# Mixing stage of a decoder layer: TensorE's order taken from the source, the recurrence spread over the projections

## The chip, the cores and the metric

The kernel runs on one core of one Trainium2 chip. The metric is the device time of one execution in microseconds. Three timed executions of the kernel before gave 2511.76, 2511.89 and 2522.68 us; the median is 2511.89 us. The engines are named as the profile names them: PE is TensorE's matmuls (PEld its weight loads), DVE is VectorE, ACT is ScalarE, POOL is GpSimd and SP is SyncE, which issues every DMA of this kernel in one queue.

## The reference, cut to what matters

One decoder layer on 1024 tokens of width 1024, in f32. The change lies in its middle part, the mixing:

```
h = rms(x); proj = h @ w_in
# columns: [q | f | v | out gate | pool input | merge gate A | merge gate B]
f = lb + (1 - lb) * sigmoid(f_r);  k = 1 - f;  q = silu(q_r)
# 8 heads, state 128x128 each, over time:
S_t = diag(f_t) S_{t-1} + k_t outer v_t;   o_t = S_t^T q_t
o   = rms(o) * silu(og);            y_a = o @ w_branch_a
# 4 channel groups, trailing means over 2, 4, 8, 16 positions minus the token:
mixed = (pooled @ pool_w) * pool_scale;  y_b = mixed @ w_branch_b
x  += (sigmoid(ga) * y_a + sigmoid(gb) * y_b) @ w_out
```

A SwiGLU feed-forward stands before it and another behind it, then a gated embedding and a last norm. Those parts are the same in both kernels.

## The kernel before, in words

**Tiling.** Activations are kept with the feature on the 128 partitions and tokens along the row, as tiles of 512 tokens (a "half"). Every f32 operand of a projection is split in a high and a low part (`split`, L117: a cast on ACT, then the difference on DVE), and a product is three matmuls of 128x512 (`mm3`, L148). I call one 128x512 matmul a *product row*.

**A pair of column blocks.** `pair` (L294) computes two blocks of 128 output columns at once with seven block products instead of eight; each is 12 product rows. Products 1 and 2 come first, then the two that the pair before left over (`rest`, 4 and 3, run by `flush`), then 6, 5, 7. Between them ACT copies banks out (L330, L341, L344) and DVE adds (L81). The weights of a pair are loaded (`raw`), added and subtracted on POOL (L90, L93) and split into `wa`, `ws`, `wd`, `wt`. The tile pools are small (`ROOM`, L32): 12 tiles for weights, 28 for activations, 8 and 5 of half width.

**The mixing stage** (L681 to L999) runs 4 pairs for v (`v_pair`), 8 for q and f (`qf_pair`), 4 for the output gate (`og_pair`), 2 for the pooling input (`pool_pair`) and 8 for the merge gates (`gate_pair`). The results of v, of the gates and of pooling go to DRAM and are loaded back where they are used.

**The recurrence** (`hgrn`, L806) is done for each of 8 heads in two halves, 16 times in all. In one half TensorE does small f32 matmuls in groups of four, one group per bank "aux" (three banks): scores on the diagonal (L822), a transpose of v (L829), seven *levels* (L849), a transpose of k (L875), state updates (L879), the output (L897, L899), and a last transpose (L910), which I call the *turn*. In the profile such a group of four shows as 8 matmul records (4 for a transpose). Each level reads q and k as the level before left them: after a group DVE copies scores out (`copy_predicated`, L852) and multiplies q and k in place (`mul(both, both, by)`, L87 `qk<-qk,tot`), and only then can the next level's matmuls go. Before the turn ACT squares four times (L902), DVE and POOL make a reciprocal root (L161, L162), and DVE scales (L904).

**What sets the order.** In both kernels the instructions of every engine stand in one fixed order when the program runs, and each engine waits at the head of its own row. In the kernel before, a scheduler makes that order for all engines at build time, from priorities in source order and its own estimate of when things are ready. The source runs for each head: the next `qf_pair`, every second time `v_pair` and `og_pair`, then the two halves of `hgrn`, then one or two of `others` (L914). Means of the pooling groups are one function, `pool_group` (L751), called when a group's input is complete. At the end come the four `m` tiles (L936), `branch_b` for 8 column blocks with `load_act` between (L984), and the branch A pairs.

## Time and profile before

| | us |
|---|---|
| median of three timed executions | 2511.89 |
| the profiled execution, its own time | 2514.3 |
| its span, first to last instruction | 2512.6 |
| PE busy | 2363.0 (94%) |
| DVE busy | 1554.5 (62%) |
| ACT busy | 974.3 (39%) |
| POOL busy | 446.2 (18%) |
| mean granted TensorE clock | 0.975 of full |

The profiled execution took 2.4 us more than the median, and its span is 1.7 us short of its own time. Its timeline has the mixing stage from 726 us (first product row of its first pair, beside the second half of the norm) to about 1660 us. The first recurrence group starts at 824 us, the last one at 1518 us, and the last product row of branch B starts at 1558 us. "PE busy" is no measure of useful work: the records of neighbouring matmuls overlap, so waits are read from the view of waits (who waited for whom) and from the number of matmuls in a stretch of time. "PEclk" is the clock that was granted to TensorE.

### The profile page before, as it was taken

To read this page: it belongs to the slowest core of one execution; us is meant where nothing else is said; L and a number is where in the kernel's file an instruction comes from. 1 tells how busy PE (TensorE), PEld (TensorE's weight loads), DVE (VectorE), ACT (ScalarE), POOL (GpSimd) and SP (SyncE) were. 2 spreads that over 40 slices of the span, in tenths; PEclk is the share of its full clock that TensorE was granted. 3 is DMA by queue.
4 is the path that set the end of the run, shared out by engine and by line. 5 is a ranking of instruction groups with operands and counts; after the bars stand their busy time and mean duration, and the time that the engine had idled before them with its cause. 6 is when DMAs were issued, how large, how long until landed. Compare 5 with 4: busy or idle time off the path is not lost.

```text
span 2512.6 us, 29499 instructions
## 1 busy us (share of the span) xinstructions
PE 2363.0 (94%) x11003; PEld 1925.0 (77%) x11003; DVE 1554.5 (62%) x2138; ACT 974.3 (39%) x1511; POOL 446.2 (18%) x390
## 2 busy tenths in 40 slices
PE   7899999999998999989999988989899999999987
PEld 5688788877777778768778767867688888877776
DVE  5745555577776665674564675576645544577767
ACT  7433333332274334233333332236433333343375
POOL 2222322100013212122222101201322222000000
PEclk9999999999998999999999989999999999999999
DMA  5244444463432213222312346753235533644234
GB/s 206 93 155 157 157 171 147 166 227 118 126 122 84 87 48 108 69 87 82 101 61 83 117 138 211 229 196 126 101 109 164 176 103 98 239 164 139 93 107 153
DMA packets 133952, 334.11 MB, mean 133 GB/s; under 512 B 15280, under 2 KB 15792, under 8 KB 133808
## 3 DMA queue, kind: packets, MB, share of 16 engines
q1 hardware_dynamic: 133808, 332.23, 39.3%
q8 instruction: 86, 1.41, 0.2%
q14 instruction: 58, 0.48, 0.1%
HBM read 230.98 MB, written 101.19 MB: 132 GB/s over the span
## 4 chain that ended last, share of the span: by engine, by line
PE 73%; DVE 12%; ACT 4%; DMA 4%; issue 3%; POOL 3%; SPq 0%; POOLq 0%; DVEq 0%; ACTq 0%
PE pA L151 12%; PE pA L152 11%; PE pA L150 11%; PE pB L151 5%; PE pB L152 5%; PE pB L150 5%; PE aux L849 4%; PE pC L151 3%; PE pC L152 3%; PE pC L150 3%; PE aux L152 2%; PE aux L151 2%; PE aux L150 2%; DVE qk L87 1%; DVE rB L84 1%
## 5 line engine op out<-in xcount | busy, mean ns | idle before, releaser
L90 POOL TENSOR_TENSOR s<-rb 128x512 f32<-128x512 f32 x74 | 101.8, 1376 | 690.4 <-PE pA L152 355.0
L119 DVE TENSOR_TENSOR wtl<-rb,wth 128x1024 fp32r<-128x1024 f32 x74 | 90.7, 1225 | 154.3 <-ACT wth L118 151.4
L118 ACT CAST wsh<-s 128x1024 fp32r<-128x1024 f32 x74 | 77.8, 1051 | 227.4 <-POOL s L93 216.1
L93 POOL TENSOR_TENSOR rb<-ra,s 128x512 f32<-128x512 f32 x74 | 96.7, 1307 | 381.5 <-DVE wd L119 373.1
L849 PEld LDWEIGHTS aux<-qk 128*128 128x128 f32 (+1 forms) x896 | 107.6, 190 | 46.0 <-issue 28.7
L118 ACT CAST wth<-rb 128x1024 fp32r<-128x1024 f32 x74 | 77.6, 1048 | 157.9 <-POOL rb L93 157.9
L118 ACT CAST w2h<-rB 128x1024 fp32r<-128x1024 f32 x72 | 68.6, 976 | 177.0 <-DVE rB L84 152.8
L849 PE MATMUL aux<-qk 128*128 128x64 f32 (+1 forms) x896 | 115.1, 273 | 18.4 <-DVE qk L87 17.3
L119 DVE TENSOR_TENSOR wsl<-s,wsh 128x1024 fp32r<-128x1024 f32 x74 | 90.5, 1223 | 65.0 <-ACT wsh L118 54.3
L150 PE MATMUL pA<-xT1h,wsh 128*128 128x512 f32 x280 | 112.6, 402 | 17.6 <-ACT xT1h L118 17.6
L118 ACT CAST wah<-ra 128x1024 fp32r<-128x1024 f32 x74 | 77.9, 1053 | 127.5 <-PE pC L151 79.2
L150 PE MATMUL pA<-xT3h,wth 128*128 128x512 f32 x296 | 118.7, 401 | 3.7 <-ACT g L341 2.4
L150 PE MATMUL pB<-xT1h,wsh 128*128 128x512 f32 x296 | 117.5, 397 | 2.8 <-DVE o L81 1.1
L152 PE MATMUL pB<-xT1h,wsl 128*128 128x512 f32 x296 | 118.5, 400 | 0.0
L150 PE MATMUL pC<-x0h,wah 128*128 128x512 f32 x296 | 116.9, 395 | 1.5 <-ACT x0h L118 1.3
L152 PE MATMUL pA<-x0h,wal 128*128 128x512 f32 x296 | 116.6, 394 | 1.8 <-DVE wal L119 1.7
L151 PE MATMUL pB<-xT1l,wsh 128*128 128x512 f32 x296 | 117.5, 397 | 0.3 <-DVE xT1l L119 0.3
L151 PE MATMUL pC<-x0l,wah 128*128 128x512 f32 x296 | 116.7, 394 | 0.9 <-DVE x0l L119 0.9
L151 PE MATMUL pA<-xT3l,wth 128*128 128x512 f32 x296 | 117.4, 397 | 0.0
L150 PE MATMUL pA<-x0h,wah 128*128 128x512 f32 x296 | 117.3, 396 | 0.0
L211 POOL TENSOR_TENSOR rs<-rs,mhalf 128x1 f32<-128x1 f32 x16 | 10.7, 667 | 600.4 <-DVE rs L210 600.4
L152 PE MATMUL pA<-xT3h,wtl 128*128 128x512 f32 x296 | 117.1, 396 | 0.0
(338 smaller groups left out, 6768.8 us busy)
## 6 DMA issues: line engine op xcount, KB each, us to landing
ra<-in_ffn_w_dram SPq DMA_DIRECT2D x50, 512.0 KB, 3.7
rb<-in_ffn_w_dram SPq DMA_DIRECT2D x44, 512.0 KB, 4.0
gsS<-gs SPq DMA_DIRECT2D x88, 256.0 KB, 2.2
rB<-in_ffn_w_dram SPq DMA_DIRECT2D x40, 512.0 KB, 4.3
gr<-gsS SPq DMA_DIRECT2D x40, 512.0 KB, 4.3
gsA<-g SPq DMA_DIRECT2D x66, 256.0 KB, 2.0
gr<-gsA SPq DMA_DIRECT2D x30, 512.0 KB, 4.0
ra<-in_w_in_dram SPq DMA_DIRECT2D x29, 512.0 KB, 3.7
```

Source lines behind the costliest of these rows:

```text
L84: nc.vector.tensor_tensor(o, x, y, ALU.subtract)
L87: nc.vector.tensor_tensor(o, x, y, ALU.mult)
L90: nc.gpsimd.tensor_tensor(o, x, y, ALU.add)
L93: nc.gpsimd.tensor_tensor(o, x, y, ALU.subtract)
L118: nc.scalar.copy(hi, src)
L119: nc.vector.tensor_tensor(lo, src, hi.bitcast(F32), ALU.subtract)
L150: nc.tensor.matmul(ps, ah, bh, start=first, stop=False, **kw)
L151: nc.tensor.matmul(ps, ah, bl, start=False, stop=False, **kw)
L152: nc.tensor.matmul(ps, al, bh, start=False, stop=last, **kw)
L211: nc.gpsimd.tensor_tensor(rs, rs, mhalf[:, :1], ALU.pow)
L849: nc.tensor.matmul(ps[:m, c, :64], kc[c][:, :m], right, start=True, stop=True)
```

## The change

- **TensorE's order in the mixing is the source's.** The heads' part is put in `tc.manual_schedule(engines={nc.tensor.engine})`; on the other engines the scheduler still chooses. `pair`, `hgrn` and `branch_b` become generators: `yield False` stands behind each three product rows of a pair (28 such *parts* in a pair), and `hgrn` yields behind each of its 13 groups of a half. `among` deals 84 parts (88 in heads 0 and 2, 74 in head 7) evenly over a head's 26 groups.
- **The turn is put off.** It becomes a closure that runs behind the third group of the next half (`i == 2`).
- **Order of the pairs.** v goes first of the three pairs at the start (before: the q and f pairs of heads 0 and 1, then v; now v, q and f of head 0, output gate), and with heads 1, 3 and 5 run the v and output-gate pairs of the next two heads and the q-f pair of the next. The pooling pairs go with heads 0 and 2, the last two gate pairs and branch B's first block (`branch_b(0)`) with head 7.
- **Pooling means in steps.** `pool_means` yields after each half of each window step and is advanced once per part of the next pair (`beside_means`); its tiles come from the weights' pool (both halves in one tile). `pool_maps` then does the maps; `pool_w` is loaded and split twice instead of once.
- **Tiles.** The state is kept in `f`'s tile instead of a new one; `og` is loaded behind the group that updates the state (before: at the half's start); branch B's gate tile is loaded from the other half-width pool and its product is written in place, and its banks are "pA" alone (before: three "aux" and two "pA" in turn).
- **Order of DMAs.** `load` can be held behind a given DMA in SP's row (`tc.issue_after`): the `m` tiles behind what was issued last before them, and the loads behind the recurrence behind the last `og` load.

```diff
-    def load(dst, src):
-        nc.sync.dma_start(out=dst, in_=src)
+    behind, latest = [None], [None]
+
+    def load(dst, src, at_once=False):
+        with ExitStack() as turn:
+            if behind[0] is not None and not at_once:
+                turn.enter_context(tc.issue_after(behind[0]))
+            latest[0] = nc.sync.dma_start(out=dst, in_=src).ins
         return dst
...
                 mm3(ps, hi[:, c], lo[:, c], *act[b][k], start and k == 0, k == 3)
+                yield False
...
+    def beside_means(it):
+        for part in it:
+            yield part
+            while means and next(means[0], 0) == 0:
+                means.pop(0)
...
-        og = load(t_("h", "og"), og_dram[h][half])
...
+        og = load(t_("h", "og"), og_dram[h][half], True)
+        og_last[0] = latest[0]
         befores = []
-        for c, (s_, p_) in enumerate(zip(chunks(t_("h", "st")), chunks(ps))):
+        for c, (s_, p_) in enumerate(zip(chunks(f), chunks(ps))):
...
-        ps = bank("aux")
-        for p_, a_ in zip(chunks(ps), qc):
-            nc.tensor.transpose(p_, a_, ident)
-        nc.vector.scalar_tensor_tensor(og, ps, onorm[:, h : h + 1], og, ALU.mult, ALU.mult)
-        store(o_dram[h][half], og)
+        def turn():
+            ps = bank("aux")
+            for p_, a_ in zip(chunks(ps), qc):
+                nc.tensor.transpose(p_, a_, ident)
+            nc.vector.scalar_tensor_tensor(og, ps, onorm[:, h : h + 1], og, ALU.mult, ALU.mult)
+            store(o_dram[h][half], og)
+        turns.append(turn)
...
+    GROUPS = 2 * 13
+    def head(h):
+        for half in range(2):
+            for i, _ in enumerate(hgrn(h, half)):
+                if i == 2 and turns:
+                    turns.pop(0)()
+                yield
+    def among(its, groups, n):
+        parts = (p for it in its for p in it if not p)
+        done = 0
+        for i, _ in enumerate(groups, 1):
+            while done * GROUPS < i * n:
+                next(parts, None)
+                done += 1
+        for _ in parts:
+            pass
...
-            ps = bank(BANKS_B[n_b[0] % len(BANKS_B)], "yb")
+            ps = bank("pA", "yb")
...
+    with tc.manual_schedule(engines={nc.tensor.engine}):
+        for h in range(HEADS):
+            its = more[h]() if h in more else (v_pair(h + 1), qf_pair(h + 1), og_pair(h + 1))
+            among(its, head(h), (74 if h == 7 else 3 * PAIR + 4 * (h in (0, 2))))
+        turns.pop(0)()
+    behind[0] = og_last[0]
```

TensorE, between the two halves of head 0 in the kernel before. `pC` rows are product rows of a pair, `aux` rows are recurrence groups; the turn of the first half (L910) stands 11 product rows behind that half's output matmuls:

```order
L150 MATMUL pC_6549<-x0h_5391,wah_6528 128x512
L151 MATMUL pC_6549<-x0l_5392,wah_6528 128x512
L910 MATMUL aux_6300<-ident,qk_5509 128x128 x4
L822 MATMUL aux_6312<-qk_5510 128x128 x4
L829 MATMUL aux_6318<-ident,v_6308 128x128 x4
L152 MATMUL pC_6549<-x0h_5391,wal_6529 128x512
L150 MATMUL pC_6549<-x0h_5411,wah_6528 128x512
L151 MATMUL pC_6549<-x0l_5412,wah_6528 128x512
L152 MATMUL pC_6549<-x0h_5411,wal_6529 128x512
L150 MATMUL pC_6549<-x0h_5431,wah_6528 128x512
L849 MATMUL aux_6333<-qk_5510 128x64 x4
L151 MATMUL pC_6549<-x0l_5432,wah_6528 128x512
```

The same engine in the changed kernel, second half of head 1, from its first level (now L886) to the second, with the turn (now L957) of the first half (`qk_6233`) behind the level:

```order
L886 MATMUL aux_7057<-qk_6234 128x64 x4
L957 MATMUL aux_7062<-ident,qk_6233 128x128 x4
L157 MATMUL pA_6933<-xT1h_5766,wsh_6920 128x512
L158 MATMUL pA_6933<-xT1l_5767,wsh_6920 128x512
L159 MATMUL pA_6933<-xT1h_5766,wsl_6921 128x512
L157 MATMUL pA_6933<-xT1h_5795,wsh_6920 128x512
L158 MATMUL pA_6933<-xT1l_5796,wsh_6920 128x512
L159 MATMUL pA_6933<-xT1h_5795,wsl_6921 128x512
L157 MATMUL pB_7040<-xT1h_5636,wsh_6920 128x512
L158 MATMUL pB_7040<-xT1l_5637,wsh_6920 128x512
L159 MATMUL pB_7040<-xT1h_5636,wsl_6921 128x512
L886 MATMUL aux_7081<-qk_6234 128x64 x4
```

Two neighbouring levels had mostly 4 to 6 product rows between them and now have 9 or 12 (6 at some places of head 7). Between a half's output matmuls and its turn stood 10 to 14 product rows in 13 of the 16 halves; now 24 or more product rows and three small groups stand there, 18 product rows for the last half. Runs of recurrence groups without a product row between fell away, and the blocks of small matmuls among product rows rose from 173 to 193.

TensorE at the end of the recurrence, head 7's second half, in the kernel before; `yb` is branch B:

```order
L910 MATMUL aux_10727<-ident,qk_9871 128x128 x4
L822 MATMUL aux_10739<-qk_9872 128x128 x4
L829 MATMUL aux_10745<-ident,v_10735 128x128 x4
L849 MATMUL aux_10760<-qk_9872 128x64 x4
L849 MATMUL aux_10767<-qk_9872 128x64 x4
L849 MATMUL aux_10774<-qk_9872 128x64 x4
L849 MATMUL aux_10781<-qk_9872 128x64 x4
L849 MATMUL aux_10788<-qk_9872 128x64 x4
L150 MATMUL pC_11461<-x0h_11306,wah_11440 128x512
L849 MATMUL aux_10795<-qk_9872 128x64 x4
L151 MATMUL pC_11461<-x0l_11307,wah_11440 128x512
L152 MATMUL pC_11461<-x0h_11306,wal_11441 128x512
```

The end of the same half in the changed kernel, with branch B's first block around the output matmuls:

```order
L943 MATMUL aux_11004<-f_9861,qk_9859 128x128
L941 MATMUL aux_11004<-v_10790,score_5506 128x128
L943 MATMUL aux_11004<-f_9861,qk_9859 128x128
L941 MATMUL aux_11004<-v_10790,score_5506 128x128
L943 MATMUL aux_11004<-f_9861,qk_9859 128x128
L157 MATMUL yb_10992<-mh_10691,wb_10987 128x512
L158 MATMUL yb_10992<-ml_10692,wb_10987 128x512
L159 MATMUL yb_10992<-mh_10691,wb_10987 128x512
L157 MATMUL yb_10992<-mh_10705,wb_10987 128x512
L158 MATMUL yb_10992<-ml_10706,wb_10987 128x512
L159 MATMUL yb_10992<-mh_10705,wb_10987 128x512
L157 MATMUL yb_11023<-mh_10684,wb_10987 128x512
```

Head 7's second half had only a handful of product rows among its groups; its levels now lie among the last gate pair's.

DVE in the pooling of head 2's time, changed kernel, from within one window step (`pw`, L81) to the multiplication of a level (`pb` and `pwhl` are the splits for the maps):

```order
L81 TENSOR_TENSOR pw_7758<-pw_7740 128x4
L87 TENSOR_TENSOR pw_7758<-pw_7758,invc 128x8
L799 SCALAR_TENSOR_TENSOR o_7321<-pw_7758,o_7321 128x504
L84 TENSOR_TENSOR o_7321<-pw_7758,o_7321 128x8
L799 SCALAR_TENSOR_TENSOR o_7322<-pw_7758,o_7322 128x512
L81 TENSOR_TENSOR f_7523<-f_7523,pB_7663 128x512
L119 TENSOR_TENSOR pwhl_7776<-pwr_7774,pwhl_7776 128x512
L119 TENSOR_TENSOR pb_7779<-o_7324,pb_7779 128x512
L718 TENSOR_SCALAR f_7523<-f_7523,lb_126,lb 128x512
L119 TENSOR_TENSOR pb_7788<-o_7323,pb_7788 128x512
L890 COPY_PREDICATED score_5506<-mask_81,aux_7753 128x64x4
L87 TENSOR_TENSOR qk_6906<-qk_6906,tot_7685 128x2x64x4
```

In the kernel before, all window steps of a group stand in DVE's row one behind the other, with the turn's scaling among them. In the changed kernel they stand between levels, but at this place 13 other DVE rows still lie between one level's multiplication and the next level's score copy.

More of the change, by code (lines that the diff above doesn't have):

```diff
@@ L288, in hybrid_block, with flushed @@
     waiting = []
+    def flushed():
+        while waiting:
+            yield from waiting.pop(0)()
     def flush():
-        while waiting:
-            waiting.pop(0)()
+        for _ in flushed():
+            pass
     def pair(wa, wb, act, tiles, on11, on22, on21, on12, early=False):
@@ L348, in rest @@
         def rest():
-            product(4, pa, False)
+            yield from product(4, pa, False)
             on21(pa)
-            product(3, pb, False)
+            yield from product(3, pb, False)
             add(c2, c2, pb)
@@ L357, in steps @@
     def steps(it, n=9):
-        for _ in range(n):
-            if next(it, 0) == 0:
+        for end in it:
+            n -= end
+            if not n:
                 return
@@ L366, in run_pair @@
         if not starts:
-            steps(pair(*args, **kw))
+            yield from pair(*args, **kw)
             return
@@ L738, in done @@
             store(og_dram[h + i][half], t)
-        out_pair(w_in[OG + h], w_in[OG + h + 1], act, done)
+            og_there.add((h + i, half))
+        yield from out_pair(w_in[OG + h], w_in[OG + h + 1], act, done)
     def gate_pair(at, j, dst):
@@ L745, in done, with pool_means @@
             store(dst[j + i][half], t)
-        out_pair(w_in[at + j], w_in[at + j + 1], act, done)
-    pw_split = []
-    def pool_group(g, u):
+        yield from out_pair(w_in[at + j], w_in[at + j + 1], act, done)
+    means, pooled = [], []
+    def beside_means(it):
[3 more added lines that the diff above has]
+                means.pop(0)
+        while means:
+            for _ in means.pop(0):
+                pass
+    def pool_means(g, u):
         win = 2 << g
@@ L773, in pool_group, with pool_maps @@
             )
-        if not pw_split:
-            r = t_("h", "pwr")
-            load(r.rearrange("p (g d) -> p g d", g=NG), a["pool_w"].rearrange("g c d -> c g d"))
-            pw_split.append(hilo_half(r, "w", "pwhl"))
-        wh, wl = pw_split[0]
-        gc = slice(g * P, (g + 1) * P)
-        for half in range(2):
-            ph, pl = hilo_half(u[half], "w", "pb")
-            ps = bank("aux")
-            mm3(ps, wh[:, gc], wl[:, gc], ph, pl, True, True)
-            nc.scalar.mul(u[half], ps, pscale[:, g : g + 1])
-            store(m_dram[g][half], u[half])
+            yield
+        pooled.append((g, u))
+    def pool_maps():
+        r = t_("h", "pwr")
+        load(r.rearrange("p (g d) -> p g d", g=NG), a["pool_w"].rearrange("g c d -> c g d"))
+        wh, wl = hilo_half(r, "w", "pwhl")
+        while pooled:
+            g, u = pooled.pop(0)
+            gc = slice(g * P, (g + 1) * P)
+            for half in range(2):
+                ph, pl = hilo_half(u[half], "w", "pb")
+                ps = bank("aux")
+                mm3(ps, wh[:, gc], wl[:, gc], ph, pl, True, True)
+                nc.scalar.mul(u[half], ps, pscale[:, g : g + 1])
+                store(m_dram[g][half], u[half])
+                yield False
     def pool_pair(g):
@@ L816, in hgrn @@
         nc.scalar.activation(k, f, AF.Copy, scale=-1.0, bias=1.0)
-        v = load(t_("h", "v"), v_dram[h][half])
-        og = load(t_("h", "og"), og_dram[h][half])
+        v = load(t_("h", "v"), v_dram[h][half], True)
         ps = bank("aux")
@@ L829, in hgrn @@
             nc.tensor.transpose(p_, v_, ident)
+        yield
         nc.scalar.copy(v, ps)
@@ L921, in hybrid_block @@
-    qf_pair(0)
-    for h in range(HEADS):
-        if h < HEADS - 1:
-            qf_pair(h + 1)
-        if h % 2 == 0:
-            v_pair(h)
-            og_pair(h)
-            flush()
-        for half in range(2):
-            hgrn(h, half)
-        others.pop(0)()
-        if h in (1, 3):
-            others.pop(0)()
-    m_parts = []
-    for g in range(NG):
-        m = t_("q", "m")
-        for half, c in enumerate((L, R)):
-            load(m[:, c], m_dram[g][half])
-        m_parts.append(halves(hilo(m, "a", "m")))
@@ new lines, in among, with around @@
+    def among(its, groups, n):
[6 more added lines that the diff above has]
+        for _ in parts:
+            pass
+    PAIR = 28
+    def around(first, acts, *its):
+        yield first
+        next(acts)
+        for it in its[:-1]:
+            yield it
+        next(acts)
+        yield its[-1]
+    more = {
+        0: lambda: (pool_pair(0), beside_means(qf_pair(1)), pool_maps(),
+                    gate_pair(GB, 0, gb_dram)),
+        2: lambda: (pool_pair(2), beside_means(qf_pair(3)), pool_maps(),
+                    gate_pair(GB, 2, gb_dram)),
+        4: lambda: (qf_pair(5), gate_pair(GB, 4, gb_dram), gate_pair(GB, 6, gb_dram)),
+        6: lambda: (qf_pair(7), gate_pair(GA, 0, ga_dram), gate_pair(GA, 2, ga_dram)),
+        7: lambda: around(gate_pair(GA, 4, ga_dram), act_b(), gate_pair(GA, 6, ga_dram), flushed(),
+                          branch_b(0)),
+    }
@@ L946, in branch_b, with act_b @@
+    for it in (v_pair(0), qf_pair(0), og_pair(0)):
+        steps(it)
+    m_parts = []
+    def act_b():
+        behind[0] = latest[0]
+        for g in range(NG):
+            m = t_("q", "m")
+            for half, c in enumerate((L, R)):
+                load(m[:, c], m_dram[g][half])
+            m_parts.append(halves(hilo(m, "a", "m")))
+        m_last, behind[0] = latest[0], None
+        yield True
+        behind[0] = m_last
+        yield True
     def branch_b(j):
@@ L982, in load_act @@
         put(("T3", "T2"), hilo(b2, "a", "xT3"))
-    for j in range(KC):
-        branch_b(j)
+    for j in range(1, KC):
+        steps(branch_b(j))
         if j % 2:
             load_act(j // 2)
+    behind[0] = latest[0]
     for j in range(0, KC, 2):
@@ L1071, in hybrid_block @@
     act = rest_of(x)
+    behind[0] = None
     ffn_up(act, a["ffn2_w1"], a["ffn2_w3"], gs_dram,
```

72 lines of the change are left out of this document (36 added, 36 removed).

## The prediction

> **What bounds the kernel now.** I read the page first, then the busy times by stretch, then the waits of TensorE (PE) inside the stretches, then the timeline at two of these waits. From the page: the span, DVE's busy share, and the chain that ended last by engine:
>
> ```profile
> span 2512.6 us, 29499 instructions
> PE 2363.0 (94%) x11003; PEld 1925.0 (77%) x11003; DVE 1554.5 (62%) x2138; ACT 974.3 (39%) x1511; POOL 446.2 (18%) x390
> PE 73%; DVE 12%; ACT 4%; DMA 4%; issue 3%; POOL 3%; SPq 0%; POOLq 0%; DVEq 0%; ACTq 0%
> ```
>
> PE carries the chain, so what the change can win is time in which PE waits or runs at a lower clock. By stretch (busy us of PE, PEld, DVE, ACT, POOL with instruction counts, then the granted clock, DMA share, GB/s):
>
> ```profile
> 790.00:1480.00 690.00, 654.58 (x3532) 538.10 (x3532) 424.38 (x705) 250.32 (x481) 143.79 (x106) 1.00 0.27 90
> 1480.00:1530.00 50.00, 35.81 (x155) 30.37 (x154) 28.61 (x51) 11.63 (x30) 5.89 (x5) 0.69 0.39 129
> 1160.00:1215.00 55.00, 55.00 (x244) 45.55 (x243) 22.04 (x26) 21.91 (x31) 15.45 (x12) 1.00 0.31 99
> 1075.00:1100.00 25.00, 19.38 (x89) 14.99 (x88) 20.74 (x55) 9.31 (x21) 1.38 (x2) 0.86 0.32 111
> ```
>
> The third row holds products alone and nothing waits in it: 55.00 / 244 = 0.225 us for one 128x512 matmul, which I call a product row. DVE is busy 424 of 690 us in the recurrence's stretch, so it isn't full; it is late only where its row stands in a bad order. PE's waits in that stretch (us in total, times, longest):
>
> ```profile
> PE aux L849 <- DVE qk L87: 11.4, 13, 1.5
> PE aux L910 <- DVE qk L904: 10.0, 9, 2.5
> PE aux L910 <- DVE tot L87: 3.9, 4, 1.4
> PE pA L150 <- ACT o L344: 2.7, 4, 0.9
> PE aux L150 <- ACT pb L118: 1.9, 1, 1.9
> PE pA L152 <- DVE wal L119: 1.5, 1, 1.5
> PE pA L150 <- ACT qk L341: 1.3, 2, 0.7
> PE aux L829 <- DMA v<-v_dram: 1.0, 1, 1.0
> PE aux L910 <- DVE o L84: 0.7, 1, 0.7
> PE pA L150 <- ACT f L344: 0.4, 1, 0.4
> PE pC L150 <- ACT wah L118: 0.2, 1, 0.2
> ```
>
> Together 35.0 us: 11.4 before levels (L849), 10.0 + 3.9 + 0.7 = 14.6 before the turn (L910), 9.0 before products and v. So the change can win little elsewhere in this stretch.
>
> **The change part by part.**
>
> *Levels.* The time from one level to the next is a DVE answer: score copy, then the multiplication in place. Mean ns of one in DVE's groups from 790 to 1530 us, and one wait in the timeline:
>
> ```profile
> L87 DVE TENSOR_TENSOR qk<-qk,tot 128x512 f32<-128x512 f32 x96 | 74.2, 773 | 17.7 <-PE aux L849 17.1
> L852 DVE COPY_PREDICATED score<-mask,aux 128x256 f32<-128x256 uint16 x80 | 44.5, 556 | 58.4 <-PE aux L849 57.3
> L119 DVE TENSOR_TENSOR wal<-ra,wah 128x1024 fp32r<-128x1024 f32 x24 | 30.4, 1267 | 12.8 <-ACT wah L118 6.3 <-PE pB L151 3.5 <-PE pA L152 2.0
> L81 DVE TENSOR_TENSOR pw<-o 128x511 f32<-128x511 f32 x8 | 5.5, 683 | 0.0
> ```
>
> ```profile
> 836.32 1.00 PE L849 MATMUL aux<-qk 128*128 128x64 f32 x8
> 837.45 0.39 PE L152 MATMUL pC<-x0h,wal 128*128 128x512 f32 x1
> 837.34 1.39 DVE L87 TENSOR_TENSOR tot<-tot 128x128 f32<-128x128 f32 x6
> 838.64 0.72 DVE L852 COPY_PREDICATED score<-mask,aux 128x256 f32<-128x256 uint16 x1
> 839.16 0.72 DVE L87 TENSOR_TENSOR qk<-qk,f 128x512 f32<-128x512 f32 x1
> 840.03 1.08 PE L849 MATMUL aux<-qk 128*128 128x64 f32 x8 [1.26 <-DVE qk L87]
> ```
>
> Copy and multiplication take 0.56 + 0.77 = 1.33 us; from the multiplication's end (839.88) to PE's next start are 0.15 us, so an undisturbed answer needs about 1.5 us. Six product rows between levels are 6 x 0.225 = 1.35 us: short by a little even then, and by 1.26 us where DVE first does foreign rows (`tot`), as here. The new order leaves 9 or 12 rows, 2.0 or 2.7 us. That takes an undisturbed answer and 0.5 to 1.2 us of foreign DVE work; one 1.27 us low part (`wal`) in front can still overshoot 9 rows by some tenths. I put the 11.4 us at 2.0: minus 9.4. The rows in that place are products which PE has to do anyhow.
>
> *The turn.* What lies between a half's output and its turn is seen whole at the end of the recurrence:
>
> ```profile
> 1514.35 0.53 PE L899 MATMUL aux<-st,qk 128*128 128x128 f32 x2
> 1514.98 0.28 ACT L902 ACTIVATE qk<-aux 128x128 f32<-128x128 f32 x1 [2.50 <-PE aux L899]
> 1516.15 0.17 DVE L161 TENSOR_SCALAR rso<-rso 128x4 f32<-128x4 f32 x1 [2.29 <-ACT qk L902]
> 1516.46 1.01 POOL L162 TENSOR_TENSOR rso<-rso,mhalf 128x4 f32<-128x4 f32 x1 [33.32 <-DVE rso L161]
> 1517.50 0.69 DVE L904 TENSOR_TENSOR qk<-aux,rso 128x512 f32<-128x512 f32 x1 [1.18 <-POOL rso L162]
> 1518.34 1.09 PE L910 MATMUL aux<-ident,qk 128*128 128x128 f32 x4 [3.46 <-DVE qk L904]
> ```
>
> 3.46 us with ACT, DVE and POOL free. Before, mostly 11 product rows (2.5 us) stood in this place: a wait of about 1 us each, and 14 such waits of 14.6 us in all are in the list. Now at least 24 product rows (5.4 us) and three small groups stand there, 18 rows (4.1 us) at the very end. POOL's root would have to come 2 us late to matter, behind a weight sum in its row. Minus 14.6.
>
> *Head 7.* In 1480 to 1530 us PE did 155 matmuls: 49 product rows (17 + 16 + 16 on L150 to L152, below) and 106 small ones.
>
> ```profile
> 1480.00:1530.00 50.00, 7.47 (x17) 3.69 (x17) 0.69 0.39 129
> 1480.00:1530.00 50.00, 7.22 (x16) 3.58 (x17) 0.69 0.39 129
> 1480.00:1530.00 50.00, 6.78 (x16) 3.44 (x16) 0.69 0.39 129
> ```
>
> A small one costs 0.11 us at full clock (the 8 of the level at 836.32 and one product row are through by 837.45: (1.13 - 0.225) / 8). So 49 x 0.225 + 106 x 0.11 = 22.7 us of work took 50: 27.3 us are lost, to waits in the chain of levels without products between and to a clock of 0.69. Now the same groups lie among 74 parts of the last gate pairs and branch B's first block. The clock was 1.00 over 790 to 1480 with waits of up to 2.5 us strewn in, so I expect it back at full here. What stays: 6 to 9 product rows per level, with splits of `m`, branch B's weights and `load_act` crowding DVE's row (five low parts and one scaling among the first two levels, some 5 us of DVE work against 3 us on PE). I leave 4.0 us: minus 23.3.
>
> *Products, v and pooling.* Of the 9.0 us a third (the pool maps' 1.9 and `wal`'s 1.5 in the same crowd) should go with the means in steps: minus 3. The clock of 0.86 in 1075 to 1100 us is worth 0.14 x 25 = 3.5 us at most, where a wait of 2.5 us stands: minus 2.5. Against that, in head 2 DVE has 13 other rows between two levels: nine of half width at 0.68 (the `pw` row) and four small ones at 0.17 (the `rso` row), 6.8 us. With the answer before it (1.5) and its own (1.5) the next level can go 9.8 us after the group before; PE has 21 product rows and a small group to do in that time, 5.6 us. It waits some 4 us, and the maps and the gate pair's `wal` stand in the same crowd, with products queued behind them. Plus 5 there, plus 1 in head 0, where the windows are shorter.
>
> *More blocks.* 193 instead of 173 blocks of small matmuls: no row prices a boundary alone; between nothing and the 0.15 us of a handoff, 0 to 3 us; I take 2.
>
> *At nothing:* the second load and split of `pool_w` (one DMA, one ACT and one DVE row) stands under qf products. The `og` load moves behind the state's group, ahead of a use some 9 us later (the turn's rows above); a DMA of its size lands in about 2 us, weights in about 4:
>
> ```profile
> gsS<-gs SPq DMA_DIRECT2D x88, 256.0 KB, 2.2
> ra<-in_w_in_dram SPq DMA_DIRECT2D x29, 512.0 KB, 3.7
> ```
>
> But all loads share SP's row, so an `og` load that waits for its tile holds the next weights. Behind the last `og` load are now held branch B's weights, `load_act` and branch A's weights. Cover: branch B's 15 further products, 15 x 12 x 0.225 = 41 us. If that cover fails, the first product waits for a whole load, split and sum, some 8 us. The state in `f`'s tile and branch B's banks move no bound. The stage's begin (v first) keeps its three pairs and their chain: 0, between -5 and +3.
>
> *Sum.* -9.4 - 14.6 - 23.3 - 3 - 2.5 + 6 + 2 = -44.8 us. Against the profiled execution (2514.3; its span is 2512.6) that is 2469.5; this execution lies 2.4 above the median of the timed ones, 2511.9, so I predict 2467.
>
> [...] By the row, a wait of 2.5 us was enough to bring the clock to 0.86 in its 25 us. [...]
>
> **The rivals.** *All of it goes and more:* if the spacing covers every DVE answer and the pile-ups hide, the 35.0, the 27.3 and 2.5 us vanish against 2 for blocks, with a little at the stage's begin: 2512 - 63 - 5 = 2444. For it: DVE is busy 62% only. Against it: the crowd in DVE's row in heads 2 and 7.
>
> *The waits move:* with the rows of PE fixed in source order, a pair's copies (`L344`, 0.9 us at longest) and low parts could hold products. 26 pairs at 1.5 us each are 39 us, and with the sum above 2506. For it: 9.0 us of such waits exist. Against it: the pair's own order of products is unchanged, and more small groups now lie in it, so each split has more time.
>
> *Slower:* DVE answers late at nearly every level. DVE's order is still chosen at build time, and if it sets a foreign row of 1.3 us in front of the usual 1.5 us, each answer misses the 2.0 us. 96 level-to-level steps (16 halves, six each) at the 0.9 us of the present waits (11.4 / 13) are 86 us in place of 2: 2467 + 84 = 2551, more with the clock down as in 1480 to 1530. It decides from a mean wait of (44.8 + 12.6 + 2) / 96 = 0.62 us per step. Against it: in the order most steps have copy and multiplication side by side. [...]
>
> **How the numbers follow.** About 0.5% (12.6 us) is what a measurement of this kernel can tell from no change. Forecast (2450 to 2490) 0.71; all of it (2440 to 2450) 0.11; waits move (2499 to 2524) 0.09; slower 0.09. Faster by over 0.5%, below 2499: 0.82; within: 0.09; slower: 0.09. The range leaves out the slower case and most of the moved waits: 2440 to 2497, its upper end being the sum with the 8 us of failed cover, 3.5 us of clock, 3 us at the begin and some 15 us of new level waits.
>
> **What would show it.** Right: waits before L957 near nothing; before L886 below 4 us; the clock near 1.00 from the first to the last group; no stretch like 1480 to 1530; PE's remaining waits in head 2's pooling and head 7. Wrong: waits before L886 in most of 96 steps; `wal`, `wsl` or a DMA ending PE's waits; a clock below 0.95 over the recurrence; a long wait before branch A's first products.

## The result and the profile after

Seven executions of the changed kernel have a median of 2499.43 us (2496.93 to 2504.48), seven of the kernel before, beside them, 2514.85 us (2511.76 to 2522.68). The ratio is 0.9933, with an interval of 0.9916 to 0.9949: about 17 us faster. Forecast were 45 us, and the time lies 2.4 us above the range. The profiled execution has a span of 2495.1 us, 17.5 less than before.

PE is busy 94% as before, DVE and ACT 62% and 39%, so the page's shares tell nothing of the change. The stretches do (same columns as in the prediction; the first two rows are the recurrence's stretch and the end of head 7 before, the third is the begin of the stage, and the last is that begin in the kernel before):

```profile
790.00:1480.00 690.00, 656.29 (x3560) 547.57 (x3559) 429.35 (x721) 249.67 (x487) 145.33 (x109) 0.99 0.26 87
1480.00:1530.00 50.00, 48.49 (x235) 39.82 (x234) 33.02 (x49) 18.44 (x33) 4.86 (x4) 1.00 0.79 262
734.00:790.00 56.00, 39.17 (x167) 29.63 (x166) 35.98 (x42) 25.04 (x32) 16.22 (x13) 0.85 0.22 72
...
734.00:790.00 56.00, 44.88 (x189) 34.46 (x188) 41.10 (x48) 28.61 (x39) 18.60 (x14) 0.85 0.16 57
```

In the 50 us from 1480 PE now starts 235 matmuls instead of 155, at full clock. In the 690 us before that it starts only 28 more than before, and the clock is 0.99 instead of 1.00. At the stage's begin it starts 22 fewer. PE's waits in that long stretch (us in total, times, longest):

```profile
PE aux L865 <- DMA v<-v_dram: 14.1, 4, 4.1
PE aux L886 <- DVE qk L87: 11.8, 17, 3.0
PE aux L886 <- DVE tot L87: 2.8, 3, 0.9
PE aux L158 <- DVE pb L119: 2.4, 1, 2.4
PE aux L886 <- ACT pb L118: 0.8, 1, 0.8
PE aux L886 <- ACT o L761: 0.5, 1, 0.5
...
```

Together 33.2 us with two smaller rows of 0.5 and 0.3, against 35.0 before. The turn's 14.6 us are no longer in the list, and of the products' waits only the pooling maps' 2.4 us (`pb`) are left. But 14.1 us stand in a row that had 1.0: the transposes of `v` wait for a DMA, four times. And the levels (L886) wait 11.8 + 2.8 + 0.8 + 0.5 = 15.9 us, where 11.4 were; 3.6 of them stand in head 7's second half, which in the kernel before lay behind 1480.

Why `v` is late is read from SP's row. The second of the four waits, at the begin of head 2, stands for all: first SP's DMAs, then PE's rows.

```profile
957.44 0.33 SPq L149 DMA_DIRECT2D ra<-in_w_in_dram  x1
959.78 0.33 SPq L149 DMA_DIRECT2D rb<-in_w_in_dram  x1
...
970.01 0.33 SPq L153 DMA_DIRECT2D og_dram<-o  x1
984.56 0.33 SPq L149 DMA_DIRECT2D ra<-in_w_in_dram  x1
986.90 0.33 SPq L149 DMA_DIRECT2D rb<-in_w_in_dram  x1
987.28 0.42 SPq L149 DMA_DIRECT2D v<-v_dram  x1
```

```profile
991.89 0.74 PE L865 MATMUL aux<-ident,v 128*128 128x128 f32 x4 [3.61 <-DMA v<-v_dram]
992.31 0.76 PE L157 MATMUL pC<-x0h,wah 128*128 128x512 f32 x1
```

SP issues nothing from 970.3 to 984.6: at the head of its row stands `ra` of the next head's second pair, which waits until POOL has done with the weight tile that it is to take (the longest of SP's waits for `POOL rb` is 14.1 us). `v` stands behind it and behind `rb`, is issued at 987.3 and lands at 991.9, although nothing else held it (run 5 below issues it right behind the `og` store). Behind the wait the clock is halved as well: 3.2 us of the view by stretches, with a granted clock of 0.50. In this trace's half-clock stretches neighbouring product rows start 0.43 us apart (median), at full clock 0.23.

```profile
992.40:995.60 3.20, 3.20 (x10) 2.52 (x9) 0.00 (x0) 0.59 (x1) 0.00 (x0) 0.50 0.00 0
```

### The profile page after: what moved, and what is told of

Read it like the earlier page. It is cut to its first block, busy times and chain, and to the rows that moved or that the text cites. A ratio compares the mean times of both kernels' runs of the same rounds, so it can differ in the third digit from the quotient of the medians.

```text
span 2495.1 us, 29437 instructions
## 1 busy us (share of the span) xinstructions
PE 2351.3 (94%) x11003; PEld 1922.5 (77%) x11003; DVE 1554.2 (62%) x2139; ACT 975.5 (39%) x1512; POOL 445.2 (18%) x390
## 4 chain that ended last, share of the span: by engine, by line
PE 71%; DVE 13%; DMA 5%; ACT 4%; issue 4%; POOL 3%; SPq 0%; DVEq 0%; POOLq 0%; ACTq 0%
PE pA L158 11%; PE pA L157 11%; PE pA L159 11%; PE pB L157 5%; PE pB L158 5%; PE pB L159 5%; PE pC L158 3%; PE pC L159 3%; PE pC L157 3%; PE aux L886 3%; PE aux L159 2%; PE aux L158 2%; PE aux L157 2%; DVE tot L87 1%; DVE qk L87 1%
## 5 line engine op out<-in xcount | busy, mean ns | idle before, releaser
L886 PEld LDWEIGHTS aux<-qk 128*128 128x128 f32 (+1 forms) x896 | 107.5, 184 | 39.4 <-issue 17.6
L886 PE MATMUL aux<-qk 128*128 128x64 f32 (+1 forms) x896 | 110.0, 266 | 16.2 <-DVE qk L87 11.8
L157 PE MATMUL pC<-x0h,wah 128*128 128x512 f32 x296 | 122.0, 412 | 1.3 <-ACT x0h L118 1.3
L159 PE MATMUL pC<-x0h,wal 128*128 128x512 f32 x296 | 118.2, 399 | 0.0
L158 PE MATMUL pA<-x0l,wah 128*128 128x512 f32 x296 | 115.9, 392 | 2.5 <-DVE x0l L119 2.5
L157 PE MATMUL pB<-x,wth 128*128 128x512 f32 x296 | 118.0, 399 | 0.0
```

The costliest lines, as they stand in the source:

```text
L157: nc.tensor.matmul(ps, ah, bh, start=first, stop=False, **kw)
L158: nc.tensor.matmul(ps, ah, bl, start=False, stop=False, **kw)
L159: nc.tensor.matmul(ps, al, bh, start=False, stop=last, **kw)
L886: nc.tensor.matmul(ps[:m, c, :64], kc[c][:, :m], right, start=True, stop=True)
```

## Theory, rival and the experiments

**Theory.** The written order does what it was forecast to do at the turn and at head 7. What it won was given back at places where another engine's row is in a bad order: `v` in SP's (14.1 us and the clock behind it), the third pair's rows in DVE's at the begin, and in DVE's row the levels' answers, which are longer than I took them for. **Rival.** PE's fixed order only moves waits: whatever is mended, the next row waits instead.

All numbers of an experiment are set against the changed kernel. Where only some microseconds matter I use the *recurrence time*: from the first half's first group to the last half's. The view of that source line has both ends; of the changed kernel it is

```profile
L857 PE MATMUL aux<-qk x128: 270/275/275, 810.7 to 1456.7; 128*128 128x128 f32 x128
```

1456.7 - 810.7 = 646.0 us. It holds the same rows of PE in all kernels below, but for a turn or five parts where that is said, and it leaves out the rest of the kernel, which differs by some microseconds from one execution to the next. Runs 2, 3, 4, 7, 8, 9 and 10 are one execution each.

### 1. v ahead of the weights

```diff
         v = load(t_("h", "v"), v_dram[h][half], True)
+        if half == 0 and h % 2 == 0:
+            behind[0] = latest[0]
```

> The changed kernel with one order added in SP's row: v's load for the first half of heads 0, 2, 4 and 6 stands ahead of the next pair's two weight loads instead of behind them. Nothing else is edited. Theory (the v loads arrive late because they queue behind two weight loads that wait for POOL): TensorE's waits for v fall from 14.1 us in 4 to under 2, and nothing takes their place; the time falls by 9 to 14 us, to about 2487. Rival (TensorE's rows are in a fixed order and DVE's answers behind v are late anyway, so the wait only moves to the next row): the waits for v go, the waits before the levels or the products grow by as much, and the time stays within 4 us of 2499.

Measured: 2519.3 us median, ratio to before 1.0011 (0.9995 to 1.0026): no gain over the kernel before, some 20 us worse than the changed one. Recurrence time 663.8 us. The waits for `v` are gone, all of them, and these stand there (790 to 1560 us):

```profile
PE aux L888 <- DVE qk L87: 14.2, 18, 2.9
PE pA L159 <- DVE wal L119: 8.5, 4, 2.1
PE pA L157 <- ACT wah L118: 8.4, 4, 2.1
PE aux L888 <- ACT qk L711: 5.6, 2, 3.3
...
```

A miss, and it looks like the rival: 16.9 us of waits for weights, in four heads. SP's row shows what I had overlooked:

```profile
976.43 0.38 SPq L149 DMA_DIRECT2D v<-v_dram  x1
976.91 0.40 SPq L149 DMA_DIRECT2D ra<-in_w_in_dram  x1
993.65 0.32 SPq L153 DMA_DIRECT2D og_dram<-o  x1
994.03 0.42 SPq L149 DMA_DIRECT2D rb<-in_w_in_dram  x1
```

The `ra` and `rb` that the changed kernel issues at 957 and 960 belong to the first pair of the next head. In the source they stand behind `v`, and the scheduler had drawn them 27 to 30 us ahead of it. My edit forbade that, so this pair's weights came 20 and 34 us later than before (6 us of each because this execution was already that much behind). The edit was too strong for the question; run 5 asks it again.

### 2. Another order of the first three pairs

```diff
-    for it in (v_pair(0), qf_pair(0), og_pair(0)):
+    for it in (qf_pair(0), og_pair(0), v_pair(0)):
```

> The changed kernel with another order of the first three pairs: q and f of head 0, output gate, v (in place of v, q and f, output gate). Theory (the stage's begin lost some 7 us because the third pair's output-gate rows stand in DVE's row ahead of the norm's last rows, and the norm's transposes wait for these): the wait before the norm's transposes falls from 8.1 us to about 4 and the one before the first xT1h products from 7.4 to about 4.5; the span falls by 4 to 8 us, to about 2489. Rival (the begin is longer because v comes first and the other two pairs have less to run beside the norm): with v last the waits are the same or longer, and the span stays within 3 us of 2495 or grows.

Measured: span 2493.6 us, recurrence time 808.4 to 1449.3, 640.9 us. Waits from the begin of the stage to the first group:

```profile
PE tr L249 <- DVE t L199: 5.9, 1, 5.9
PE pA L157 <- ACT xT1h L118: 4.7, 2, 2.7
PE pA L158 <- DVE xT1l L119: 2.2, 2, 1.6
```

In the changed kernel these are 6.0 + 2.1 (`tr`), 7.4 and 1.2. From the first product row of the stage to the first group it is 808.4 - 729.3 = 79.1 us, in the changed kernel 810.7 - 726.4 = 84.3: 5.2 less with the same rows of PE. The recurrence time is 5.1 less because head 0's wait for `v` (3.7 us, and clock behind it) is gone. The span shows only 1.5 of this: this execution was 2.9 us late when the stage began, and lost some 6 more behind the recurrence.

So order matters here by the 5 us expected, but the wait that I had named is only partly the cause: the one of 6 us before the norm's transposes stays. What probably went is seen in DVE's row of the changed kernel:

```profile
758.80 0.69 DVE L81 TENSOR_TENSOR o<-o,pC 128x512 f32<-128x512 f32 x1 [4.97 <-PE pC L159]
760.18 0.69 DVE L87 TENSOR_TENSOR o<-o,sg 128x512 f32<-128x512 f32 x1 [0.70 <-ACT sg L752]
760.79 0.74 DVE L199 SCALAR_TENSOR_TENSOR t<-tr,ngains,b 128x512 f32<-128x512 f32 x1
```

With the output gate third, DVE stands 5 us at the head of its row for a product bank while the norm's `t` rows, which all later splits need, are queued behind it. With v third no row of DVE there stands more than 0.7 us. That this stand is the whole 5 us is argued from the trace; the run shows only that the order of the pairs decides.

### 3. The turn at once

```diff
             for i, _ in enumerate(hgrn(h, half)):
-                if i == 2 and turns:
-                    turns.pop(0)()
                 yield
+            if turns and (h, half) != (7, 1):
+                turns.pop(0)()
```

> The changed kernel with the turn put back: it runs at the end of its own half, 9 to 12 product rows behind the output, in place of behind the third group of the next half (the last half's turn stays). Theory (putting off the turn is worth the 14 us that it saved): the waits before the turn are 12 to 15 us in 13 to 15 waits, and the span is 2505 to 2512. Rival (with the groups spread evenly DVE is free at the turn, so the delay earns little): under 5 us of waits, a span below 2501.

Measured: span 2514.8 us; recurrence time 669.7 us, 23.7 more (one turn more lies in it). Waits from 790 to 1480 us:

```profile
PE aux L957 <- DVE qk L949: 23.7, 15, 2.3
```

The rival falls. The theory was too small: with the groups spread evenly every turn waits, for 23.7 / 15 = 1.6 us, where before 14 waits had 1.0 us each. Putting off the turn is worth more in this order than in the old one.

### 4. and 8. POOL's sums left out

With run 1's edit (4) and without it (8); the products of the heads' part take the raw weights in place of sums and differences:

```diff
-            s = t_("w", "s1")
-            pool_add(s[:, L], rb[:, L], rb[:, R])
-            pool_sub(s[:, R], s[:, L], ra[:, L])
+            s = rb if no_sums[0] else t_("w", "s1")
...
-            pool_sub(rb[:, L], ra[:, L], rb[:, L])
-            pool_sub(rb[:, R], ra[:, R], s[:, R])
```

> As the first of these (v ahead of the weights), and the sums of weights on POOL (four 128x512 rows for each pair) are left out in the heads' part; the products take the raw weights in place of the sums, so the output isn't the reference's. Theory (the multiplication of q and k in place takes 1.7 us instead of 0.69 where a POOL sum runs beside it, and small products of f 1.2 instead of 0.17): no such row takes over 0.8 us, and the waits before the levels fall by 5 to 7 us against the first of these. Rival (the levels wait for foreign DVE rows, whatever POOL does): they fall by under 2 us.

> The changed kernel, nothing moved, but the sums of weights on POOL left out in the heads' part (the products take the raw weights, so the output isn't the reference's). Theory (POOL's rows stretch the rows of DVE that run beside them, and that makes half of the waits before the levels): these waits fall from 15.4 us to 6 to 10, no multiplication of q and k takes over 0.8 us, and v's load, whose weight loads then wait less for POOL, comes earlier too; the span falls to 2478 to 2488. Rival (the levels wait for foreign rows): the waits before the levels fall by under 3 us.

Measured: 4 has a span of 2495.2 us and a recurrence time of 638.2 us, 25.6 less than run 1; 8 has 2461.0 and 615.3 us, 30.7 less than the changed kernel and more than expected (a span of 2478 to 2488). In 4 the waits before the levels fall from 23.0 us in run 1 to 8.7 (790 to 1480 us), more than expected too; its waits for weights stay. The multiplications of q and k between levels, in the changed kernel and in 8 (790 to 1530 us):

```profile
L87 DVE TENSOR_TENSOR qk<-qk,tot 128x512 f32<-128x512 f32 x96 | 77.9, 812 | 25.4 <-PE aux L886 25.2
L87 DVE TENSOR_TENSOR tot<-tot 128x128 f32<-128x128 f32 x16 | 9.5, 593 | 0.5
```

```profile
L87 DVE TENSOR_TENSOR qk<-qk,tot 128x512 f32<-128x512 f32 x96 | 66.4, 692 | 34.1 <-PE aux L888 34.0
L87 DVE TENSOR_TENSOR tot<-tot 128x128 f32<-128x128 f32 x16 | 4.6, 288 | 0.3
```

The 0.81 us of the mean is a mixture: 16 of the 96 rows take 1.0 to 1.74 us, the others some 0.69, and without POOL's sums none takes over 0.75. What one such row does to PE (first the three rows of the changed kernel, then PE's answer):

```profile
955.89 0.42 DVE L890 COPY_PREDICATED score<-mask,aux 128x256 f32<-128x256 uint16 x1
956.12 1.30 POOL L93 TENSOR_TENSOR rb<-ra,s 128x512 f32<-128x512 f32 x1 [7.75 <-DVE wd L119]
956.22 1.74 DVE L87 TENSOR_TENSOR qk<-qk,tot 128x512 f32<-128x512 f32 x1
958.11 1.08 PE L886 MATMUL aux<-qk 128*128 128x64 f32 x8 [0.35 <-DVE qk L87]
```

POOL's sum begins 0.1 us ahead of the multiplication and ends at 957.42; the multiplication ends 0.54 us behind that, about its own length. It doesn't run slower, it stands until POOL has done: all 16 long rows end 0.54 or 0.55 us behind a POOL sum. In 8 the waits before the levels (L888) are 4.7 us for `qk`, 1.2 and 0.8 for the pooling splits and 0.7 for an output copy, none for `tot`: 7.4 in place of 15.9 us. So more than half of what the levels wait goes with POOL's rows. In the changed kernel's trace 3.6 us of it stand right behind a multiplication that was held, and 2.8 behind `tot` rows that were held (1.2 to 1.3 us in place of 0.2 to 0.3). The larger part of 8's gain is `v`: without the sums its waits fall from 14.1 to 3.6 us, the longest to 1.2, and the four half-clock stretches behind them, of 3.4 us each, are gone; counted at half of their length, an estimate from the granted clock of 0.50, that is 6.8 us. With the 8.5 us of the levels that makes 25.8 of the 30.7 us; the rest stands in no wait of the list.

### 5. v ahead of the second pair's weights only

```diff
         def raw(src, s):
+            if v_there:
+                v_there[1] -= 1
+                if v_there[1] < 0:
+                    with tc.issue_after(v_there[0]):
+                        return load(t_("w", s), src)
             return load(t_("w", s), src)
...
+        if half == 0 and h % 2 == 0:
+            v_there[:] = [latest[0], 2]
```

> The changed kernel with a weaker order in SP's row: in heads 0, 2, 4 and 6 only the weight loads from the head's second pair on stand behind v's load; the first pair's, which the first attempt held back too, may go ahead of it. Theory (v is late only because of the second pair's two weight loads; the first attempt lost its gain because the first pair's weights, otherwise loaded some 27 us earlier, then came late): TensorE's waits for v fall from 14.1 us to under 3, no waits for wah or wal take their place, and the time falls by 9 to 14 us against the changed kernel. Rival (whatever moves v earlier moves weights later, since SP's row and the weight tiles are the limit): waits for weights of 5 us or more appear, and the time stays within 4 us of the changed kernel.

Measured: 2477.15 us median, ratio to before 0.9829 (0.9812 to 0.9846). Recurrence time 811.7 to 1435.1, 623.4 us: 22.6 less than the changed kernel. SP's row at the same place, and PE's waits from 790 to 1480 us, which have no row for `v` and none for weights any more:

```profile
965.30 0.33 SPq L153 DMA_DIRECT2D og_dram<-o  x1
965.72 0.38 SPq L149 DMA_DIRECT2D v<-v_dram  x1
979.84 0.33 SPq L149 DMA_DIRECT2D ra<-in_w_in_dram  x1
```

```profile
PE aux L893 <- DVE qk L87: 10.8, 16, 2.5
PE aux L893 <- DVE tot L87: 2.7, 3, 0.9
PE aux L158 <- DVE pb L119: 2.4, 1, 2.4
...
```

The theory holds and the rival falls: `v` could be issued right behind the `og` store, which in the changed kernel is at 970.0 and 17 us earlier than `v` went; the weights lost nothing by standing behind it, and no other wait grew (a copy's 1.1 us in this stretch stood behind 1480 before). The gain is larger than the 9 to 14 us expected, because behind each wait there were also 3.4 us at half clock: 14.1 us of waits and four times 1.7 us, half of each stretch, are 20.9 of the 22.6 us.

### 6. Both

> The same order of v's load, together with the first three pairs in the order q and f of head 0, output gate, v. Theory (the two losses are separate): the begin of the stage loses some 5 us less than in the changed kernel and the waits for v are gone; together 14 to 18 us below the changed kernel, a ratio to the kernel before of 0.985 to 0.988. Rival (head 0's v comes from the third pair now, so its load is late again): a wait for v of 3 us or more in head 0 stays, and the sum is under 10 us.

Measured: 2473.57 us median, ratio 0.9811 (0.9788 to 0.9835). No wait for `v` in head 0 or elsewhere. From the stage's first product row (731.5) to the first group (809.9) it is 78.4 us, 5.9 less than in the changed kernel; the recurrence time is 624.6 us. In run 5 the same stretch took 84.6 us. So in the traces the two losses are separate and add; the timed ratios of runs 5 and 6 overlap in their intervals and don't show it by themselves.

### 7. and 11. TensorE's order left to the scheduler

```diff
-    with tc.manual_schedule(engines={nc.tensor.engine}):
+    with ExitStack():
```

7 is the changed kernel with this edit, 11 has run 5's as well.

> The changed kernel with TensorE's order in the heads' part left to the scheduler again; the pairs' order, the turn put off, the means in steps and the loads stay as changed. Theory (the turn and the end of head 7 need the order written out): some of the waits before the turn and between head 7's levels return, and the span is 2503 to 2520. Rival (the gain comes from the turn put off and from branch B beside head 7, whoever makes the order; the scheduler also sees when v and the weights land and puts other rows ahead of them): the waits for v are under 4 us and the span is within 6 us of 2495 or below it.

> v's load ahead of the second pair's weights, and TensorE's order left to the scheduler. Theory (all that the order from the source cost was the wait for v and the clock behind it, so with v in time the two orders are equal): within 5 us of the same kernel with the order from the source, 2472 to 2482, a ratio of 0.982 to 0.985. Rival (the scheduler's order also avoids waits before levels that the fixed spacing has): 2460 to 2470, a ratio below 0.980.

Measured: 7 took 2477.41 us in its one execution, span 2475.7, recurrence time 627.3 us. 11 has a median of 2469.75 us, a ratio of 0.9825 (0.9805 to 0.9845), and a recurrence time of 617.1 us. Waits of 7 from 790 to 1560 us:

```profile
PE aux L886 <- DVE qk L87: 6.5, 12, 1.2
PE aux L865 <- DMA v<-v_dram: 5.1, 4, 1.8
PE aux L886 <- DVE tot L87: 2.8, 3, 0.9
...
```

For 7 the theory fell: the turn waits 2.0 us in all, head 7's last levels 0.8 us. Neither needs the order to be written out, and without it the kernel is 20 us faster. A part of the reason can be counted in PE's row. SP's row is the same as in the changed kernel (`v` behind `ra` and `rb`), but the scheduler reckons with that: in heads 0, 2, 4 and 6 it puts 22 product rows between the first group and the transposes of `v`, where the written order has 12, and as many as the written order in the other halves. Ten rows are 10 x 0.225 = 2.25 us, and the longest wait falls from 4.1 to 1.8 us; only one of the four has a half-clock stretch behind it (3.4 us from 1328.0). That is 9.0 us of waits and 5.1 of clock, of 18.7 us over the recurrence. The levels wait 10.1 instead of 15.9 us, which I haven't followed further. With `v` in time (11 against 5) the two orders' ratios are equal within their intervals, 0.9825 and 0.9829. In the two profiles the scheduler's is 6 us shorter over the recurrence, with 6.8 us instead of 10.8 before the levels; by the timed executions that isn't settled.

### 9. Head 7 without branch B's block

The first block of branch B and the loads and splits of `m` stand behind the recurrence; 64 parts are dealt in head 7.

```diff
-        7: lambda: around(gate_pair(GA, 4, ga_dram), act_b(), gate_pair(GA, 6, ga_dram), flushed(),
-                          branch_b(0)),
+        7: lambda: (gate_pair(GA, 4, ga_dram), gate_pair(GA, 6, ga_dram), flushed()),
```

> The changed kernel with head 7 as sparse as its own pairs make it: only the last two gate pairs stand beside it (64 parts dealt in place of 74); branch B's first block and the loads and splits of m come behind the recurrence. Theory (a part of the 22 us won at head 7 is due to branch B's rows and the early m): from head 7's second half to the end of branch B the kernel loses 15 to 25 us in place of 9, mostly where branch B begins; span 2500 to 2510. Rival (the gate pairs alone are cover enough, and branch B's block is worth nothing): the loss there is within 3 us of 9, the span 2493 to 2499.

Measured: 2511.78 us, span 2509.7. The recurrence time is the same, 646.1 us, though with five parts (15 product rows, 3.4 us) fewer in it: the waits for `v` are 1.7 us longer in this execution, and the half-clock stretch behind the last of them lasts 6.8 instead of 3.4 us. One wait has appeared, where branch B begins:

```profile
PE yb L157 <- ACT wb L118: 12.5, 1, 12.5
```

From the last half's first group (1456.7 in the changed kernel, 1457.6 here) to the first product of the output projection (1614.7 and 1631.7) it is 16.1 us longer, 3.4 of them the five parts that moved here. Head 7's own levels keep their cover (1.7 us of waits before them in its second half, 3.6 in the changed kernel): the gate pairs alone do that. The theory holds. What branch B's block and the early `m` are worth is the seam behind it.

### 10. Means at once

```diff
-                    means.append(pool_means(g + k, [got.pop((k, 0)), got.pop((k, 1))]))
+                    for _ in pool_means(g + k, [got.pop((k, 0)), got.pop((k, 1))]):
+                        pass
```

> The changed kernel with the pooling means at once, as each group's input is complete, in place of in steps beside the next pair. Theory (steps keep DVE's foreign rows apart): waits before the levels in heads 0 and 2 grow by 5 us or more, the span is 2500 or more. Rival (the scheduler sets DVE's order anyway, and in steps the rows collide with the maps and the next pair's weights): no more than 2 us either way, or even less waiting, a span of 2490 to 2497.

Measured: span 2501.4 us, recurrence time 649.6 us, 3.6 more. One level waits 8.4 us for the pooling split; the other waits before levels fall from 15.1 to 12.8 us. All of them together grow by 5.3 us and the span by 6.3, as the theory expected; by the recurrence time the steps are worth 3.6 us in this one execution.

### 12. All three edits

The order left to the scheduler and `v` ahead (run 11's edits), and run 2's order of the first pairs.

> The same, with the first three pairs as q and f of head 0, output gate, v. Theory (the begin's loss is separate from the rest): 4 to 6 us below the one before, by a begin that loses 20 in place of 25 us. Rival (with TensorE's order free the scheduler fills the begin in any case): within 2 us of the one before.

Measured: 2464.72 us median, ratio to before 0.9801 (0.9780 to 0.9821), about 50 us below the kernel before and some 33 below the changed one (0.9801 / 0.9933 = 0.987). First product row to first group 806.6 - 727.6 = 79.0 us, as in run 2 (84.0 in run 11), and a recurrence time of 616.8 us, as in 11. The begin's 5 us are won whoever makes PE's order; the medians of 11 and 12 differ by 5.0 us too, with intervals that overlap.

## Why the prediction was wrong, point by point

**The step that failed** stands under *At nothing*. I wrote there that "all loads share SP's row, so an `og` load that waits for its tile holds the next weights", and followed what is held *by* `og`. I didn't follow `v` through the same row, though the change moves whole pairs and with them their weight loads, and though the row of waits for `v` (1.0 us, once) was in my list. It became 14.1 us of waits and, with the clock behind them, 22.6 us (run 5). Half of the forecast gain went there. The measured 2499.4 lies at the edge of the range of *the waits move* (2499 to 2524), but by luck: that rival had the copies and low parts as its mechanism, and those waits did not grow, they fell. How far the time lies outside my own range hangs on the base: from 2511.9, with the measured ratio, it would be 2495, inside. What failed is the gain, 17 of 45 us.

**The stage's begin**, put at 0 between -5 and +3, cost some 5 us: PE starts 22 fewer matmuls there than before (22 x 0.225 = 5.0), and another order of the pairs wins 5.2 us (run 2) or 5.9 (run 6). DVE stands 5.0 us at the head of its row for the output gate's bank. I kept "its three pairs and their chain", but the third pair's kind decides which DVE rows stand among the norm's.

With these two terms mended (run 6) the ratio is 0.9811, and the forecast sum's is 2469.5 / 2514.3 = 0.9822. So the rest of the sum came out, but not each term of it; errors in both directions cancel:

- *Turn*, minus 14.6: right, its waits are gone; undoing it costs 23.7 us (run 3).
- *Head 7*, minus 23.3: right in size. From 1456 to 1500 us, where its second half now stands, PE waits 5.0 us at a clock of 1.00; I had left 4.0 of the 27.3. The one large wait of the crowd that I feared (`m`'s low parts) is 3.0 us. What I took for the work of branch B's rows at the levels is done by the gate pairs; those rows pay at the seam (run 9).
- *Pooling heads*, plus 6: right in size. Beside the means' steps in heads 0 and 2 the levels wait 3.6 us, and the maps wait 2.4. Steps for the means brought 3.6 us (run 10).
- *Levels*, minus 9.4: mis-sized. Without head 7's second half (3.6 us) and the pooling heads' 3.6, 8.7 of the 15.9 us are left where I had left 2.0. I took foreign rows of DVE for the cause and built the answer of 1.33 us from means (0.56 + 0.77) without asking why the mean lies above most rows. A multiplication beside a POOL sum took up to 1.74 us in place of 0.69, and 9 rows don't cover that: 3.6 of the 8.7 us stand right behind such rows, 2.8 behind `tot` rows that POOL held, and without the sums 0.6 are left (run 8). The trace before showed it already: in 10 of its 13 waits before levels, 7.6 of the 11.4 us, the multiplication just ahead had taken 1.2 to 1.8 us.
- *Products and v*, minus 3: the products' waits fell by 5.6 us (8.0 to 2.4, which are the maps'), those of `v` rose by 13.1.
- *Clock*, minus 2.5: the half-clock stretch of 6.8 us in head 2 went with the turn's wait of 2.5 us, another of 6.8 us stands behind the pooling maps' 2.4 us, and four of 3.4 us stand behind the waits for `v`: 0.99 in place of 1.00. The section on the hardware has what the traces show of this.
- *More blocks*, plus 2: no run here shows a price for it. In waits of 790 to 1480 us the terms add up: 35.0 forecast to fall to about 14, measured 33.2. The gap of 19.2 is `v` (13.1), the levels (6.7) and head 7's 3.6, which the forecast counts in its own term, less 4.2 at the products.

That the order was written out by hand is not what won. Runs 7 and 11 have the same gain or more without it; the gain that the runs show is in the turn put off (run 3) and in what stands beside head 7 (run 9). What the small parts and their even spacing are worth by themselves, no run shows.

## What to carry to other kernels

When one engine's row is fixed by hand, the time at which its inputs land is fixed by the rows of the engines that are still scheduled: for every input of a moved group, read what stands ahead of its load in the DMA queue and what that waits for, before pricing anything else. A fixed row can't step around a late input, and the wait can cost the clock too: behind each of the changed kernel's four waits for `v` (2.7 to 4.1 us) stood 3.4 us at half clock. An order that is to be tested by holding one DMA behind another must hold no more than that one: run 1 held the first pair's weights as well and hid a 22 us gain.

## What the runs showed of the hardware

**DVE and POOL.** In the changed kernel the multiplication `qk<-qk,tot` stood still while a POOL sum that had begun before it ran: 1.74 in place of 0.69 us beside a sum of 1.30 us (lines above). The other way round the sum was held: nine sums that began behind such a multiplication took 1.58 to 1.75 us, the 18 sums of 726 to 1530 us with no DVE row beside them 1.28 to 1.30. Rows with one input from a bank weren't held: in the same stretch the 10 rows `o<-o,pB` that ran beside POOL took 0.69 us, the 26 others 0.68. The row `f<-f,lb,lb`, with one tensor of 128x512 and none from a bank, was held: the 7 that began beside a POOL sum took 0.99 to 1.52 us, the 9 others 0.54 or 0.55.

**The clock.** In each trace the half-clock stretches begin on one grid of 3.4133 us; the 37 of the kernel before and the changed kernel lie within 4 ns of it, and all but the last of each, which runs to the end of the execution, last 1 to 7 whole steps. I laid that grid over the fourteen traces of this study, from the first product rows at some 10 us on, and summed PE's gaps of over 50 ns in each step that ran at full clock. Of 178 steps with 2.0 us or more idle all were followed by a step at half clock; with 1.6 to 2.0 us 36 of 71; with 1.3 to 1.6 us 9 of 89; with 0.5 to 1.3 us 2 of 572. Of 171 half-clock steps with 0.5 us or more idle every one was followed by another, of 248 with less only 10. In the kernel before and the changed kernel alone these counts are 29 of 29, 4 of 6, 0 of 12 and 0 of 93, then 27 of 27 and 3 of 38. So what a wait cost in clock hung on where it fell on the grid: in the changed kernel the pooling maps' wait of 2.4 us, of which 2.2 lie in one step, was followed by 6.8 us at half clock, while the 3.0 us wait in head 7's second half, of which the grid puts 1.8 in one step and 1.3 in the next, had none behind it.
